# Expert weights in 4 KB rows, 256-column products, a fourth fixed expert and a shared scaling in the second of two transformer blocks

## The chip, the cores and the metric

The kernel runs on one core of a Trainium2 chip. The core has five engines that run their own instruction streams side by side: TensorE (PE in the profile; its weight loads are PEld), VectorE (DVE), ScalarE (ACT), GpSimd (POOL) and SyncE (SP), which here only issues transfers. Sixteen DMA engines move data between main memory and the core's memory. An engine runs its instructions in the order of the program and stops at the first whose inputs or buffer aren't ready. The metric is the device time of one execution in microseconds (us).

## The reference

Two transformer blocks follow one another on 1024 tokens of width 1024, all in float32. Each block is a mixer (attention and others) and a mixture of experts. Only the mixture of the second block matters here. Its routing takes, for each token, the best of four groups and in it the best two of eight experts:

```
grp = argmax(x @ wg + bg);  p_grp = softmax(...)[grp]
e_in = (x @ we + be) of that group          # 8 logits
top_v, top_i = top_k(e_in, 2);  combine = p_grp * softmax(top_v)
for each of its two experts e:              # 32 experts, hidden width 256
    y += combine * ((silu(x @ w_gate[e]) * (x @ w_up[e])) @ w_down[e])
out = h + y                                  # h: the residual
```

w_gate and w_up (w1 and w3 in the code) are 1024 x 256 for each expert, w_down (w2) is 256 x 1024.

## The kernel before, in words

**Precision.** A float32 matrix is split into a high and a low part (`w_split`, L190 on ScalarE and L194 on VectorE for weights; L1835 and L1836 for the tokens), and a product is three products of these: high by high, high by low, low by high. Experts with room for at most 64 tokens (`whole`) put the high and low tokens side by side as 128 columns of the stationary operand, so that two products do; their w2 isn't split at all.

**Experts by size.** The routing sorts the experts by the number of their tokens; position p of that order has room for `caps[p]` rows, written down in a `Lay`. The first NP positions are fixed experts, not sorted ones: their number is known when the program is built, so their weights can be loaded before the routing is known. In the second block NP is 3 with room for 128 each; position 3 has 192, then 128 three times, 96 four times, 80 six times, and 64 fifteen times. `order` says in which order they are computed: 0, 1, 2, and then a large and a small one in turn (3 and 17, 4 and 18, ...), 31 last.

**Weight tiles.** `plan_moe` queues six tiles of 128 x 1024 for each expert: four that hold two rows of 256 of w1 and two of w3 for each partition (two transfers of 256 KB each, with 2 KB contiguous in memory for each partition), and two of w2 (one transfer of 512 KB each, 4 KB contiguous). `w()` hands out the next tile. Before it does, `w_ahead` issues loads for the next LD tiles and splits the next LS. During the last row block of the mixer (`mix_out`) LD grows to 6 NP - 1, so the fixed experts' tiles are all on their way; then LD is 20 and LS is 3. A load of a sorted expert is addressed by a register that SyncE reads from `idx` (L1784), which the routing writes at L1565; SyncE issues in the order of the program, so no load passes that one. The tiles share 42 buffers of 4 KB per partition with the gathered tokens, the split tokens and weights and the outputs.

**One expert.** `gather` (L1809, GpSimd) fetches its tokens' rows. `xT` transposes and splits them. `up` (L1839) takes a tile for each quarter of the contraction and multiplies: each product (L1857) has 512 columns, 256 of w1 and 256 of w3. In the middle of it stands `hT` of the expert before, which transposes its hidden values. SiLU and the product with the other half follow (L1863 to L1869). `down` of the expert before multiplies with w2; ScalarE scales the two halves of the output by the routing weight (L1916), and `put` (L1796) adds the rows to the output with a scatter-add from GpSimd. Four steps of the rest of the routing (`route_rest`) are mixed into each expert until they are done.

**The order** of all this is the order of the program text; each engine's queue is filled by it. What comes first in the loop of `moe` (L1940 to L1957) is: gathers up to five experts ahead, `xT` of the next expert, `up`, the two w2 tiles, `down` of the expert before.

Of the kernel before, what the change touches and what calls it, by code (L numbers as in the profile page):

```python
# [14 lines left out]
OP = mybir.AluOpType  # L15
# [109 lines left out]
class Kern:  # L125
# [1644 lines left out]
    def plan_moe(self, w1, w3, w2, lay, box):  # L1770
        a1 = w1.rearrange("e (p kk k) h -> e kk p (k h)", kk=4, k=2)
        a3 = w3.rearrange("e (p kk k) h -> e kk p (k h)", kk=4, k=2)
        a2 = w2.rearrange("e (k p) d -> e k p d", k=2)
        lo, hi, al = (lambda t: t[:, 0:512]), (lambda t: t[:, 512:1024]), (lambda t: t[:, 0:1024])
        val = {}

        def src(a, p, k):
            if p < lay.NP:
                return a[p, k]

            def go(dst):
                if p not in val:
                    val.clear()
                    val[p] = self.nc.values_load(  # L1784
                        box["r"]["idx"][0:1, 2, p:p + 1], engines=[mybir.EngineType.SP], min_val=0, max_val=lay.E - 1)
                self.sy.dma_start(dst, a[bass.ds(val[p], 1), k].rearrange("o p f -> (o p) f"))
            return go
        for p in lay.order:
            for kk in range(4):
                self.w_add([(lo, src(a1, p, kk)), (hi, src(a3, p, kk))], 1024)  # L1790
            for k2 in range(2):
                self.w_add([(al, src(a2, p, k2))], 1024, None if lay.whole(p) else lay.small > 0 and not lay.add and k2 == 1)


    def put(self, ys, ix, y):
# [3 lines left out]
    def moe(self, r, vs, late=None):  # L1799
        ac, ve, te, gp = self.ac, self.ve, self.te, self.gp  # L1800
        lay = r["lay"]
# [13 lines left out]
        def xT(b):  # L1815
            X[b] = []
            for x, idn, s, n in XG.pop(b):
# [18 lines left out]
                    ve.tensor_sub(xl[:, sl], ps[:, :w], xh[:, sl])  # L1836
                X[b].append((xh, xl, s, n))

        def up(b, mid=None):  # L1839
            U = X.pop(b)  # L1840
            P = [self.p() for _ in U]
            for kk in range(4):
                if kk == 2 and mid is not None:
                    hT(mid)
                wh, wl = self.w()
                next(gen, None)
                for k in range(2):
                    for ps, (xh, xl, s, n) in zip(P, U):
                        c = 2 * kk + k
                        if xl is None:  # L1850
                            ops = [(xh[:, c].rearrange("p j n -> p (j n)"), w) for w in (wh, wl)]
                        else:
                            ops = [(x[:, c * n:(c + 1) * n], w) for x, w in ((xh, wh), (xh, wl), (xl, wh))]
                        m = 2 * n if xl is None else n
                        for j, (x, w) in enumerate(ops):
                            rhs = w[:, :1024].rearrange("p (w k h) -> p w k h", w=2, k=2)[:, :, k, :]
                            te.matmul(ps[:m].rearrange("p (w h) -> p w h", w=2), x, rhs,  # L1857
                                      start=c == 0 and j == 0, stop=c == 7 and j == len(ops) - 1)
            Hn[b] = []
            for ps, (_, xl, s, n) in zip(P, U):  # L1860
                h = self.h()
                if xl is None:
                    ac.activation(h[:n], ps[n:2 * n], AF.Copy)  # L1863
                    ve.tensor_add(h[:n], ps[:n], h[:n])
                    ac.activation(h[:n, 0:256], h[:n, 0:256], AF.Silu)
                    ve.tensor_mul(h[:n, 256:512], h[:n, 0:256], h[:n, 256:512])
                else:
                    ac.activation(h[:n, 0:256], ps[:n, 0:256], AF.Silu)
                    ve.tensor_mul(h[:n, 256:512], h[:n, 0:256], ps[:n, 256:512])  # L1869
                Hn[b].append((h, s, n))  # L1870
# [22 lines left out]
        def down(b):  # L1893
            W = WK.pop(b)
            for t, s, n in HT.pop(b):
                p0, p1 = self.p(), self.p()
                for k in range(2):
                    wh, wl = W[k]
                    if lay.whole(b):
                        m, ops = n, [(t[:, k, :], wh)]  # L1900
                    elif lay.two(b, n):
                        m, ops = 2 * n, [(t[:, k].rearrange("p j n -> p (j n)"), w) for w in (wh, wl)]
                    else:
                        hh, hl = t[:, k, 0, :], t[:, k, 1, :]
                        m, ops = n, ((hh, wh), (hh, wl), (hl, wh))
                    for j, (a, w) in enumerate(ops):
                        f, e = k == 0 and j == 0, k == 1 and j == len(ops) - 1
                        self.mm(p0[:m], a, w[:, 0:512], f, e)
                        self.mm(p1[:m], a, w[:, 512:1024], f, e)
                y = self.t()  # L1910
                for ps, o in ((p0, 0), (p1, 512)):
                    if lay.two(b, n) and not lay.add:
                        ac.activation(y[:n, o:o + 512], ps[n:2 * n], AF.Copy)
                        ve.tensor_add(y[:n, o:o + 512], ps[:n], y[:n, o:o + 512])
                    elif lay.add:
                        ac.activation(y[:n, o:o + 512], ps[:n], AF.Copy, scale=r["wc"][:n, s[1], b:b + 1])  # L1916
                    else:
                        ac.activation(y[:n, o:o + 512], ps[:n], AF.Copy)
                if lay.add:
                    self.put(ys, r["dst"][:n, s[1], b:b + 1], y[:n, :D])  # L1920
                else:
                    gp.dma_start(ys[s[0]:s[0] + n, :], y[:n, :D])

        O = lay.order
        gen = r.pop("gen")
# [11 lines left out]
        for i, b in enumerate(O):  # L1937
# [16 lines left out]
            if i:  # L1954
                down(O[i - 1])
        hT(O[-1])
        down(O[-1])  # L1957
        return ys

# [846 lines left out]
    def run(self):  # L2806
        A = self.A
        l1, l2 = self.lays = (
            Lay(2, [192] * 9 + [128] * 7, [0, 1, 9, 2, 10, 3, 4, 11, 5, 12, 6, 13, 7, 14, 8, 15], 64, False),
            Lay(3, [128] * 3 + [192] + [128] * 3 + [96] * 4 + [80] * 6 + [64] * 15,   # L2810
                [0, 1, 2] + [p + q for p in range(3, 17) for q in (0, 14)] + [31], 64, True))
        b1, b2 = {}, {}
        self.plan_one()
        self.plan_moe(A["exp_w1"][0], A["exp_w3"][0], A["exp_w2"][0], l1, b1)
        self.plan_two()
        self.plan_moe(A["w_gate_2"][0], A["w_up_2"][0], A["w_down_2"][0], l2, b2)
        self.consts()
        self.u_one()
        self.dbg("uT0", self.uh[0].bitcast(F32)[:, NM:NM + T])
        self.attn_one()  # L2820
        self.LD, self.LS = 3, 1
        self.dbg("yc0", self.ycs[0])
        self.conv_pool_in()
        self.mix_load(A["router_g"][0], A["router_e"][0], A["router_g_b"][0], A["router_e_b"][0],
                      A["norm2_g"][0], 16)
        self.merge_one()
        self.uh = self.ul = None
        vs, b1["r"] = self.mix_out(A["x"][0], A["norm2_g"][0], l1, "1")
        def gains():
            self.fg = (self.bcast(A["final_g"], D, self.t()), self.col(A["norm_mix_g_2"][0], 8))  # L2830
        ys = self.moe(b1["r"], vs, gains)
        self.moe_rest(b1["r"], vs, ys, A["exp_w1"][0], A["exp_w3"][0], A["exp_w2"][0])
        self.LS, self.LD = 1, 3
        self.join(b1["r"], ys)
        self.lru()
        self.LD, self.LS = 2, 2
        self.latents()
        self.LD, self.LS = 5, 3
        self.mix_load(A["router_group_w_2"][0], A["router_expert_w_2"][0], A["router_group_b_2"][0],
                      A["router_expert_b_2"][0], A["norm_ffn_g_2"][0], 32)  # L2840
        self.q_kv()
        self.attn_two()
        vs, b2["r"] = self.mix_out(self.x2, A["norm_ffn_g_2"][0], l2, "2", self.out[0])
        ys = self.moe(b2["r"], vs)
        self.moe_rest(b2["r"], vs, ys, A["w_gate_2"][0], A["w_up_2"][0], A["w_down_2"][0])
# [30 lines left out]
```

## Time and profile before

| | |
|---|---|
| time, median of 3 runs | 2680.14 us (2677.69 to 2683.29) |
| the profiled execution | 2676.59 us, of which the span is 2674.5 us |
| mean granted clock of TensorE | 0.97 |
| TensorE, VectorE, ScalarE, GpSimd busy | 93%, 60%, 46%, 23% |
| block two's experts | about 2290 to 2659 us of the span |

Times in the rows are microseconds from the start of the span. A row of a timeline is one or more instructions of one line, with the idle time ahead of them and what ended it in square brackets. In DMA rows `s` is the core's memory, `out<-s,dst` the scatter-add, `s<-vs,idx` the gather, and `in_w_gate`, `in_w_up`, `in_w_down` are the weights. A DMA share is the part of the sixteen engines' time that their packets took; it can be a little over 1. The granted clock is TensorE's, as a share of full speed.

### The profile page before, as it was taken

The page shows a single profiled execution, that of the slowest core. Times are in us where ns is not written, and L with a number is a line of the kernel's source. Part 1 is how long each engine was busy: PE and PEld are TensorE (multiplying, and loading weights), DVE is VectorE, ACT ScalarE, POOL GpSimd, SP SyncE. Part 2 cuts the span into 40 slices and gives each one's busy share as a digit, 9 for nine tenths or more (in the row PEclk, how much of TensorE's full clock was granted, in tenths as well). Part 3 has the DMA queues.
Part 4 walks back from the last instruction along what each step waited for, and adds up shares of the span by engine and source line. Part 5 has one row for each costly group of instructions (what it writes and reads, how often), then busy time and mean ns, then how long its engine had stood idle before and what let it go on. Part 6 is the DMA issues. An engine that isn't in the chain of part 4 may idle for free. (4 is left out here: it accounts for less than half of the span.)

```text
span 2674.5 us, 35232 instructions
## 1 busy us (share of the span) xinstructions
PE 2484.8 (93%) x12192; PEld 1912.6 (72%) x12192; DVE 1596.0 (60%) x2659; ACT 1224.4 (46%) x2153; POOL 608.1 (23%) x661
## 2 busy tenths in 40 slices
PE   7999999999999799959999999998999989689996
PEld 7976696778877577758788888996655567555543
DVE  4235338842245688765754563567776645777775
ACT  4336521131123477755344243435555532457775
POOL 1011111000001234441000002153655622223221
PEclk9999999999999899979999999998999989899998
DMA  4000243223251689852221221333222265789996
GB/s 136 25 9 10 56 144 104 83 83 103 95 181 72 197 291 311 299 195 86 63 87 48 71 79 26 94 123 113 96 96 77 76 211 178 244 249 341 344 347 218
DMA packets 245877, 378.38 MB, mean 141 GB/s; under 512 B 31344, under 2 KB 142224, under 8 KB 245696
## 3 DMA queue, kind: packets, MB, share of 16 engines
q1 hardware_dynamic: 216720, 282.42, 32.6%
q0 software_dynamic: 28976, 93.67, 11.0%
q8 instruction: 98, 1.61, 0.2%
q14 instruction: 83, 0.68, 0.1%
HBM read 296.65 MB, written 81.99 MB: 142 GB/s over the span
## 5 line engine op out<-in xcount | busy, mean ns | idle before, releaser
L216 PE MATMUL ps<-s,s 128*128 128x512 f32 (+15 forms) x8744 | 1922.4, 379 | 37.1 <-ACT s L212 7.2
L216 PEld LDWEIGHTS ps<-s,s 128*128 128x128 f32 (+6 forms) x8744 | 1502.6, 187 | 416.5 <-issue 95.1
L194 DVE TENSOR_TENSOR s<-s,s 128x1024 fp32r<-128x1024 f32 (+4 forms) x375 | 461.7, 1252 | 437.5 <-ACT s L190 402.0
L190 ACT ACTIVATE s<-s 128x1024 fp32r<-128x1024 f32 (+3 forms) x393 | 391.2, 1034 | 73.7 <-DMA s<-in_w_up 16.4
L1857 PE MATMUL ps<-s,s 128*128 128x512 f32 (+3 forms) x1200 | 319.0, 413 | 28.5 <-DVE s L194 23.3
L1857 PEld LDWEIGHTS ps<-s,s 128*128 128x128 f32 (+3 forms) x1200 | 213.8, 186 | 101.4 <-DVE s L194 36.7
L370 DVE TENSOR_REDUCE mx<-ps 128x1 f32<-128x512 f32 (+10 forms) x304 | 142.4, 505 | 17.1 <-PE ps L216 15.3
L504 ACT ACTIVATE s<-ps 128x512 f32<-128x512 f32 (+1 forms) x192 | 93.8, 489 | 114.4 <-PE ps L216 110.6
L1153 ACT ACTIVATE s<-ps 128x512 f32<-128x512 f32 x24 | 14.3, 598 | 252.0 <-PE ps L216 252.0
L519 POOL TENSOR_TENSOR s<-s,s 128x512 f32<-128x512 f32 (+1 forms) x64 | 108.3, 1692 | 48.5 <-ACT s L506 25.4
L1796 POOL DMA_INDIRECT out<-s,dst x33 | 54.0, 1635 | 244.6 <-ACT s L1916 144.5
L466 PE MATMUL ps<-s,s 128*64 128x512 f32 (+3 forms) x384 | 84.4, 521 | 0.8 <-DVE mx L370 0.8
L1046 DVE SCALAR_TENSOR_TENSOR s<-s,c,s 128x1024 f32<-128x1024 f32 x60 | 82.7, 1379 | 1.5
L1809 POOL DMA_INDIRECT s<-vs,idx x58 | 73.3, 1263 | 43.9 <-issue 10.4
L212 ACT ACTIVATE s<-s 128x512 fp32r<-128x512 f32 (+2 forms) x49 | 36.8, 775 | 76.7 <-DVE s L2329 35.6
L434 ACT ACTIVATE s<-ps 128x512 f32<-128x512 f32 (+4 forms) x112 | 49.3, 447 | 47.7 <-PE ps L216 46.6
L213 DVE TENSOR_TENSOR s<-s,s 128x512 fp32r<-128x512 f32 (+2 forms) x49 | 41.8, 890 | 45.5 <-ACT s L212 45.5
L303 ACT ACTIVATE s<-s 128x1024 f32<-128x1024 f32 (+1 forms) x25 | 26.4, 1055 | 89.1 <-DVE s L1316 46.4
L2305 ACT ACTIVATE s<-ps 128x512 f32<-128x512 f32 x16 | 9.6, 598 | 100.9 <-PE ps L216 100.9
L2352 POOL DMA_DIRECT2D g1s<-s x8 | 4.3, 539 | 226.1 <-ACT s L2306 216.9
L192 POOL TENSOR_TENSOR s<-s,s 128x1024 fp32r<-128x1024 f32 x18 | 47.1, 2618 | 32.0 <-ACT s L190 31.9
L1181 POOL DMA_DIRECT2D ms<-s x8 | 4.3, 533 | 215.9 <-DVE s L1148 161.4
(501 smaller groups left out, 2417.2 us busy)
## 6 DMA issues: line engine op xcount, KB each, us to landing
s<-in_w_in SPq DMA_DIRECT2D x80, 512.0 KB
s<-in_exp_w SPq DMA_DIRECT2D x128, 256.0 KB
s<-in_w_gate SPq DMA_DIRECT2D x128, 256.0 KB
s<-in_w_up SPq DMA_DIRECT2D x128, 256.0 KB
s<-in_w_down SPq DMA_DIRECT2D x64, 512.0 KB
s<-in_exp_w SPq DMA_DIRECT2D x32, 512.0 KB
s<-in_x SPq DMA_DIRECT2D x16, 512.0 KB
ms<-s POOLq DMA_DIRECT2D x16, 512.0 KB, 5.0
```

Of the source, the lines that this page charges most:

```text
L190: self.ac.activation(hi[:, :n], st[:, :n], AF.Copy)
L194: self.ve.tensor_sub(lo[:, :n], st[:, :n], hi[:, :n])
L216: self.te.matmul(out, lhsT, rhs, start=start, stop=stop)
L370: self.ve.tensor_reduce(mx[:, ii, j:j + 1], ps[:, c0 - s0:c1 - s0], axis=AX.X, op=OP.max)
L434: self.ac.activation(pf[:rows, c:], s[:rows, c:], AF.Exp)
L466: self.te.matmul(o[64 * hh:64 * hh + 64, c:], H["v"](j)[:rows], pf[:rows, hh, c:], start=first, stop=last and not c, skip_group_check=True)
L504: self.ac.activation(pf[:rows, hh, c:], s[:rows, c:], AF.Exp)
L519: eng.tensor_tensor(acc[:rows, :, c:], acc[:rows, :, c:], pf[:rows, :, c:], op=OP.add)
L1046: ve.scalar_tensor_tensor(a[:, :T], gl[:, k:k + T], cw[:, c, k:k + 1], a[:, :T], op0=OP.mult, op1=OP.add)
L1796: self.gp.indirect_dma_start(out=ys, out_offset=bass.IndirectOffsetOnAxis(ap=ix, axis=0), in_=y, in_offset=None, bounds_check=T - 1, oob_i ...
L1809: gp.indirect_dma_start(out=x[:n, :D], out_offset=None, in_=vs, in_offset=bass.IndirectOffsetOnAxis(ap=r["idx"][:n, j, b:b + 1], axis=0))
L1857: te.matmul(ps[:m].rearrange("p (w h) -> p w h", w=2), x, rhs, start=c == 0 and j == 0, stop=c == 7 and j == len(ops) - 1)
```

## The change

Only the second block is changed, in four places. First, w1 and w3 come in tiles of one matrix each: a transfer of 512 KB, four rows of 256 (4 KB contiguous) for each partition. An expert has six transfers instead of ten, still six tiles, and as many splits. Second, `up_add` takes these tiles in pairs (one of w1, one of w3), so that a pair holds half of the contraction; each product of 512 columns becomes two of 256, one from each tile, and `hT` of the expert before comes after the first pair. Third, four experts are fixed instead of three, each with room for 128; the position with 192 is the fifth, and the order is 0, 1, 2, 3, 17, then (4, 18), (5, 19) and so on, 31 last. Fourth, the second half of a small expert's output is scaled by VectorE from PSUM.

```diff
@@ plan_moe
+        b1, b3 = (w.rearrange("e (p kk k) h -> e kk p (k h)", kk=2, k=4) for w in (w1, w3))
...
         for p in lay.order:
+            if lay.add:
+                for a, n in ((b1, 0), (b3, 0), (b1, 1), (b3, 1), (a2, 0), (a2, 1)):
+                    self.w_add([(al, src(a, p, n))], 1024, None if a is a2 and lay.whole(p) else False)
+                continue
             for kk in range(4):
                 self.w_add([(lo, src(a1, p, kk)), (hi, src(a3, p, kk))], 1024)
             for k2 in range(2):
-                self.w_add([(al, src(a2, p, k2))], 1024, None if lay.whole(p) else lay.small > 0 and not lay.add and k2 == 1)
+                self.w_add([(al, src(a2, p, k2))], 1024, k2 == 1)
@@ moe
+        def up_add(b, U, P, mid):
+            for kk in range(2):
+                if kk and mid is not None:
+                    hT(mid)
+                W = [self.w(), self.w()]
+                for k in range(4):
+                    if k % 2 == 0:
+                        next(gen, None)
+                    c = 4 * kk + k
+                    for ps, (xh, xl, s, n) in zip(P, U):
+                        if xl is None:
+                            m, ops = 2 * n, [(xh[:, c].rearrange("p j n -> p (j n)"), o) for o in (0, 1)]
+                        else:
+                            m, ops = n, [(x[:, c * n:(c + 1) * n], o) for x, o in ((xh, 0), (xh, 1), (xl, 0))]
+                        for j, (x, o) in enumerate(ops):
+                            for h, w in enumerate(W):
+                                self.mm(ps[:m, h * 256:h * 256 + 256], x,
+                                        w[o][:, k * 256:(k + 1) * 256], c + j + h == 0,
+                                        c == 7 and h == 1 and j == len(ops) - 1)
@@ up
+            if lay.add:
+                up_add(b, U, P, mid)
+            else:
...
@@ down
+                    elif o and lay.whole(b):
+                        ve.tensor_scalar(y[:n, o:o + 512], ps[:n], r["wc"][:n, s[1], b:b + 1], None, op0=OP.mult)
                     elif lay.add:
                         ac.activation(y[:n, o:o + 512], ps[:n], AF.Copy, scale=r["wc"][:n, s[1], b:b + 1])
@@ run
-            Lay(3, [128] * 3 + [192] + [128] * 3 + [96] * 4 + [80] * 6 + [64] * 15, 
-                [0, 1, 2] + [p + q for p in range(3, 17) for q in (0, 14)] + [31], 64, True))
+            Lay(4, [128] * 4 + [192] + [128] * 2 + [96] * 4 + [80] * 6 + [64] * 15,
+                [0, 1, 2, 3, 17] + [p + q for p in range(4, 17) for q in (0, 14)] + [31], 64, True))
```

## Rows read from the trace of the kernel before

**Rows 1.** The page's busy time, share and instructions of each engine.

```profile
PE 2484.8 (93%) x12192; PEld 1912.6 (72%) x12192; DVE 1596.0 (60%) x2659; ACT 1224.4 (46%) x2153; POOL 608.1 (23%) x661
```

**Rows 2.** Busy time by window: stretch, engines PE to POOL, granted clock, DMA share, GB/s.

```profile
2287.00:2299.50 12.50, 2.34 (x16) 1.56 (x16) 9.59 (x53) 4.92 (x7) 0.58 (x1) 0.68 0.13 54
...
2310.00:2400.00 90.00, 75.87 (x341) 54.13 (x340) 66.58 (x115) 55.53 (x80) 23.36 (x16) 0.94 0.85 258
2400.00:2530.00 130.00, 122.12 (x548) 76.47 (x547) 103.54 (x131) 100.46 (x145) 37.60 (x26) 1.00 1.03 340
2530.00:2610.00 80.00, 72.30 (x312) 39.69 (x311) 56.49 (x67) 57.86 (x85) 19.86 (x15) 1.00 1.04 347
```

**Rows 3.** SyncE's load issues around the routing: start, duration in us.

```profile
2278.49 1.21 SPq L180 DMA_DIRECT2D s<-in_w_down  x2
2299.91 0.35 SPq L1786 DMA_DIRECT2D s<-in_w_gate  x1
```

**Rows 4.** Chain of waits, the first gather: start, us, what.

```profile
2299.57 6.11 DMA s<-vs,idx
```

**Rows 5.** Chain of waits at the end: the last scatter-add of the loop.

```profile
2654.42 3.52 DMA out<-s,dst
```

**Rows 6.** SyncE's issues from 2383 on.

```profile
2383.49 12.39 SPq L1786 DMA_DIRECT2D s<-in_w_down  x2
2396.79 0.33 SPq L1786 DMA_DIRECT2D s<-in_w_gate  x1
```

**Rows 7.** What SyncE waited for, 2310 to 2410: total us, times, longest.

```profile
SPq L1786 <- DMA out<-s,dst: 11.5, 1, 11.5
```

**Rows 8.** GpSimd's scatter-adds: start, us of the issue, idle before and releaser.

```profile
2470.14 1.47 POOL L1796 DMA_INDIRECT out<-s,dst  x1 [7.10 <-ACT s L1916]
...
2526.56 1.45 POOL L1796 DMA_INDIRECT out<-s,dst  x1 [7.15 <-DMA s<-in_w_up]
...
2609.72 1.42 POOL L1796 DMA_INDIRECT out<-s,dst  x1 [8.68 <-ACT s L1916]
...
2646.90 1.42 POOL L1796 DMA_INDIRECT out<-s,dst  x1 [8.18 <-DVE s L194]
```

**Rows 9.** What the engines waited for, 2530 to 2610: ScalarE's row.

```profile
ACT s L190 <- DMA s<-in_w_up: 14.4, 11, 2.8
```

**Rows 10.** DMA issues 2290 to 2660: count, median us to landing.

```profile
out<-s,dst POOLq DMA_INDIRECT x33, 8.3
```

**Rows 11.** VectorE, around one small expert.

```profile
2496.94 2.36 DVE L194 TENSOR_TENSOR s<-s,s 128x1024 fp32r<-128x1024 f32 x2 [2.02 <-ACT s L1916]
```

**Rows 12.** TensorE, the same expert's last products.

```profile
2501.42 0.97 PE L1857 MATMUL ps<-s,s 128*128 128x512 f32 x3 [0.76 <-DVE s L194]
```

**Rows 13.** DMA, 2629 to 2631: packets and rate, share of the queue.

```profile
DMA packets 448, 0.81 MB, mean 407 GB/s; under 512 B 51, under 2 KB 51, under 8 KB 448
q1 hardware_dynamic: 448, 0.81, 105.6%
```

**Rows 14.** DMA, 754 to 757: the same rows.

```profile
DMA packets 339, 1.26 MB, mean 419 GB/s; under 512 B 32, under 2 KB 32, under 8 KB 339
q1 hardware_dynamic: 339, 1.26, 103.0%
```

**Rows 15.** TensorE, 24 products of 512 columns.

```profile
2355.58 5.79 PE L1857 MATMUL ps<-s,s 128*128 128x512 f32 x24
```

**Rows 16.** ScalarE's evictions between groups of 24 products of 256 columns.

```profile
71.44 0.39 ACT L718 ACTIVATE s<-ps 128x256 f32<-128x256 f32 x1 [2.47 <-PE ps L216]
```

**Rows 17.** TensorE, 96 products of 256 columns.

```profile
1166.21 12.63 PE L216 MATMUL ps<-s,s 128*128 128x256 f32 x96
```

**Rows 18.** ScalarE by form, 2290 to 2675: busy us, mean ns, idle before.

```profile
L1916 ACT ACTIVATE s<-ps,s 64x512 f32<-64x512 f32 x32 | 21.5, 681 | 10.4 <-PE ps L216 10.3
```

**Rows 19.** VectorE by form, the same stretch.

```profile
L1864 DVE TENSOR_TENSOR s<-ps,s 64x512 f32<-64x512 f32 x15 | 10.2, 678 | 3.2 <-ACT s L1863 3.2
```

**Rows 20.** What the engines waited for, 2310 to 2400: VectorE's row.

```profile
DVE s L194 <- DMA out<-s,dst: 12.2, 3, 4.2
```

More of the change, by code (lines that the diff above doesn't have):

```diff
@@ L1841, in up @@
             P = [self.p() for _ in U]
[L1842 to L1858, printed above, removed]
+            if lay.add:
+                up_add(b, U, P, mid)
+            else:
+                for kk in range(4):
+                    wh, wl = self.w()
+                    next(gen, None)
+                    for k in range(2):
+                        for ps, (xh, xl, s, n) in zip(P, U):
+                            c = 2 * kk + k
+                            if xl is None:
+                                ops = [(xh[:, c].rearrange("p j n -> p (j n)"), w) for w in (wh, wl)]
+                            else:
+                                ops = [(x[:, c * n:(c + 1) * n], w) for x, w in ((xh, wh), (xh, wl), (xl, wh))]
+                            m = 2 * n if xl is None else n
+                            for j, (x, w) in enumerate(ops):
+                                rhs = w[:, :1024].rearrange("p (w k h) -> p w k h", w=2, k=2)[:, :, k, :]
+                                te.matmul(ps[:m].rearrange("p (w h) -> p w h", w=2), x, rhs,
+                                          start=c == 0 and j == 0, stop=c == 7 and j == len(ops) - 1)
             Hn[b] = []
```

## The prediction, made before the changed kernel was run

> **What bounds the kernel now.** I read the page's busy shares first: TensorE is busy 2484.8 us of the span [rows 1], so over the whole it is the bound. But the change touches only the experts of block two, so I cut their stretch into windows [rows 2]. There the answer differs. From 2400 to 2530 and from 2530 to 2610 the DMA share is 1.03 and 1.04: the transfers never pause. TensorE is busy 122.12 of 130 and 72.30 of 80 us. Ahead of it stand two stretches in which transfers do pause: 2287 to 2299.5 (share 0.13) and parts of 2310 to 2400 (0.85).
>
> Next the load queue's issues. The last weight load that doesn't depend on the routing is issued at 2278.49, the next at 2299.91 [rows 3]: in between SyncE has nothing to issue, because every later load is addressed by an expert number that isn't there yet. The chain of waits gives the other end of this gap: the first gather starts at 2299.57 and takes 6.11 us [rows 4], while the last scatter-add, with no loads beside it, takes 3.52 us [rows 5]. Both move 128 and 64 rows of 4 KB, so I read the difference as company on the DMA engines: the loads issued from 2299.91 on run beside the gather.
>
> The queue stands still a second time. A w2 load issued at 2383.49 holds it for 12.39 us, until 2396.79, and 11.5 us of that is a wait for a scatter-add to leave its buffer [rows 6, 7]. So every lead that loads had before is gone at 2396.8, and from there one transfer follows the other.
>
> Where TensorE feels it: the scatter-adds of the larger expert of each pair lie at 2470.14, 2526.56, 2609.72, 2646.90 [rows 8], three, four and two pairs apart. That is 18.8 us a pair, then 20.8, then 18.6. In the slow four, ScalarE waits 14.4 us for loads [rows 9]; nothing like it shows for 2400 to 2530, where the lead is being used up. Against 18.8 a pair the four lose 83.2 - 4 x 18.8 = 8.0 us. In the fast pairs what sets the pace is a ring: a scatter-add lands (8.3 us from issue, the median of 33 [rows 10]), frees a buffer, VectorE splits into it (2.36 us, after 2.02 idle), and TensorE's last three products of an expert wait 0.76 us for the next split [rows 11, 12].
>
> **The change part by part.**
>
> *A fourth fixed expert.* 24 tiles instead of 18 are loaded before the routing is known; 3.15 MB at 419 GB/s [rows 14] is 7.5 us moved into the gap, which has about 11 us free. It removes nothing from the total by itself: the load rule is "20 tiles ahead", and from the fourth tile taken on the same tile is asked for at the same point of the program as before. Whatever lead it gives, the queue's standstill at 2383.5 takes back. So 0 for the prefetch as such; its bounds are 0 and, should the lead survive, what the slow four lose beyond the next term. What it does remove is the company of the first gather: its loads are already in. 6.11 - 3.52 = -2.6 us, bounds 0 to -2.6; I take -2.6, since the nearest row (the lone scatter-add) has the same kind of transfer, and everything behind the gather shifts with it. The expert of 192 rows moves two places later in the order; the number of rows computed stays.
>
> *Four rows of 1 KB per partition.* w1 and w3 come in 4 KB runs instead of 2 KB. A stretch with only 2 KB packets of loads ran 407 GB/s at 105.6% of the engines, one with 4 KB packets 419 at 103.0% [rows 13, 14]. For 2.097 MB an expert that saves 2.097/407 - 2.097/419 in thousandths, 0.147 us, by the plain rates; brought to 100% share (385 and 407) 0.294 us. Behind the standstill some 20 experts load until 2610: -2.9 to -5.9 us, and the 8.0 us lost there are the ceiling. I take -4.5. Issues fall from ten to six an expert; SyncE waits for data anyway, so nothing for that.
>
> Here the Trainium skill speaks against the saving: DMA: Bandwidth & Descriptors, Queues, rings and completion order, has each engine drain a whole packet of one ring before it switches to another. The trace so far has scatter-adds landing in 8.3 us beside packets of 2 and 4 KB and in 3.52 alone [rows 5, 10], which agrees with sharing but says nothing of packet size. What it would make of the time is the fourth rival.
>
> *Two 256-column products for one of 512.* 672 products of 512 columns become 1344. The trace has both: 24 products of 512 in 5.79 us, 0.241 each; and groups of 24 products of 256 between two evictions, 0.39 + 2.47 = 2.86 us, 0.119 each [rows 15, 16]. Two make 0.238: -2 us over all. A row of 96 in 12.63 us [rows 17] gives 0.132, +15 us. I take 0, by the first, which is a stream of its own kind as the changed one will be; the second is kept for the range. In the stretch where loads set the pace either is hidden.
>
> *Tiles taken in pairs.* An expert's second half now needs the last split before 8 rather than 4 of its 16 old products. In the ring above that puts a second quarter, 0.97 us [rows 12], behind the split: +0.97 a pair. What stands behind it on TensorE is the down product of the expert before, and with it the scatter-add.
>
> *VectorE scales half of the small experts' output.* ScalarE's 64-row scaling is 0.681 us, VectorE's nearest operation from PSUM 0.678 [rows 18, 19]. Done side by side, the scatter-add is issued up to 0.68 earlier (bounds -0.68 and +0.68 a pair: VectorE's copy may queue behind splits). Together with the pairing I take 0 for the pairs whose pace is set by loads, and for the five exposed ones (three and two [rows 8]) 0.97 - 0.68 + a little queueing, about 0.4: +2 us, bounds 0 and +11.6 (second rival). At the very end the last expert's later half adds 0.97 and the parallel scaling takes 0.68: +0.3.
>
> *Sum.* -2.6 - 4.5 + 0 + 2 + 0.3 = -4.8 us. The profiled execution took 2676.59 us, so 2671.8 in its own terms. It lies 3.5 us below the median of the three runs (2680.14), so 2675.3 as a median.
>
> **The rivals.** A measurement of this kernel can tell about 0.2%, 5.4 us, from no change; 2674.8 and 2685.5 are the borders, and my forecast lies on the lower one.
>
> First, faster: the buffers are handed out in another order, and the load that stood at 2383.5 gets one that is free. Then the lead of 7.5 us survives, the slow four lose nothing (-8.0 instead of -4.5), and of the 12.2 us that VectorE's splits wait for scatter-adds before 2400 [rows 20] half goes. -2.6 - 8.0 - 6.1 + 2.3 = -14.4: 2666. For it: that wait is an accident of one buffer. Against: as many buffers are held as before.
>
> Second, slower: VectorE's scaling stands in its queue behind splits that themselves wait for a scatter-add, so the ring grows by 0.97 + 0.68 = 1.65, from 18.8 to 20.4 a pair. It decides as soon as the scaling starts after ScalarE's half ends. Seven pairs from 2470 to 2609.7 would take 142.8 instead of 139.6 (+3.2), the last two 40.8 instead of 37.2 (+3.6), three larger pairs before them +1.6 each (+4.8). 11.6 - 2.6 + 0.3 = +9.3: 2689. For it: VectorE is busy 103.54 of 130 us [rows 2] and the ring runs through it.
>
> Third, no change: the transfer rate beside scatter-adds and gathers is not the rate of a pure stream, the rows save nothing, and the gather's gain is spent in the ring. 0 to -2: 2679.
>
> Fourth: a scatter-add waits longer behind 4 KB packets. Two thirds of the load bytes come in packets twice as long, so a byte's packet grows by half on average; if the scatter-add's excess over the lone one, 8.3 - 3.5 = 4.8 us, grows as much, that is +2.4 a pair in the ring: 21.2 instead of 18.8. Seven pairs take 148.4 instead of 139.6 (+8.8), the last two 42.4 instead of 37.2 (+5.2), the three larger +7.2; 21.2 - 2.6 + 0.3 = +18.9: 2699.
>
> **How the numbers follow.** Forecast 0.38, its own range 2670 to 2681 and its chance cut in half by the border; first rival 0.22; second 0.23; third 0.12; fourth 0.05. Faster: 0.19 + 0.22 and 0.01 of the third, 0.42. Same: 0.19 + 0.11 = 0.30. Slower: 0.23 + 0.05 = 0.28. The range 2662 to 2691 takes in the first and second rival with a few us of their own spread, and leaves out the fourth and their far ends, some 0.17 together.
>
> **What would show it.** The gap: transfers at some 400 GB/s before 2299 and a first gather near 3.5 us. The rows: a shorter spacing of w2 loads behind 2400 and less waiting of ScalarE for loads in the slow pairs. The standstill at 2383.5: there, elsewhere or gone. The products: 48 of 256 columns in 5.7 us. The ring: fast pairs at 18.8 to 19.2; 20.4 and VectorE's scaling behind a split would be the second rival, a scatter-add median over 10 us the fourth. I am wrong in kind if TensorE's own busy time in block two grows by over 5 us, or if the early stretch changes by more than the gather's 2.6.

## The result, and the profile after

The changed kernel takes 2702.7 us (median of 6 runs, 2700.88 to 2705.8) against 2680.52: the ratio is 1.0081, 95% interval 1.0071 to 1.0091. It is 22 us slower, outside the range of the prediction. Its profiled execution took 2701.23 us, 24.6 more than that of before.

The engines' busy time on the page of the changed kernel, whose span is 2699.4 us:

```profile
PE 2496.5 (92%) x12864; PEld 1971.5 (73%) x12864; DVE 1609.4 (60%) x2674; ACT 1215.6 (45%) x2138; POOL 612.1 (23%) x661
```

The windows of [rows 2] in the changed kernel (the columns are those of the rows):

```profile
2287.00:2299.50 12.50, 2.34 (x16) 1.56 (x16) 9.29 (x52) 4.92 (x7) 0.82 (x2) 0.68 0.58 236
...
2310.00:2400.00 90.00, 74.64 (x477) 65.05 (x475) 65.69 (x110) 51.38 (x73) 19.65 (x14) 0.91 0.78 249
2400.00:2530.00 130.00, 109.12 (x651) 84.62 (x652) 88.11 (x115) 77.04 (x111) 35.76 (x23) 0.91 0.91 293
2530.00:2610.00 80.00, 74.48 (x486) 55.32 (x485) 62.67 (x73) 59.35 (x86) 22.09 (x16) 1.00 1.03 362
```

The gap is used as foretold: its share rises from 0.13 to 0.58. The slow stretch 2530 to 2610 keeps its transfers without a pause (1.03), and TensorE does more in it (74.48 us against 72.30). The loss is in the two windows between. From 2310 to 2400 the DMA share falls from 0.85 to 0.78, and from 2400 to 2530 from 1.03 to 0.91; TensorE is busy 109.12 us of 130 instead of 122.12, at a granted clock of 0.91 instead of 1.00.

What does the same work cost in all? One window from the first gather to the last scatter-add of the loop, first the kernel before, then the changed one:

```profile
2299.57:2654.42 354.85, 315.58 (x1375) 196.42 (x1376) 262.50 (x353) 248.87 (x358) 92.42 (x68) 0.97 0.96 313
```

```profile
2299.26:2679.63 380.37, 329.90 (x2049) 257.70 (x2050) 274.51 (x367) 240.76 (x344) 95.68 (x69) 0.93 0.85 284
```

The stretch is 25.6 us longer. TensorE is idle 50.5 us of it instead of 39.3, 11.2 more, and busy 14.3 us longer for the same columns, at a mean granted clock of 0.93 instead of 0.97. Busy time times clock is the same in both, 315.58 x 0.97 = 306 us and 329.90 x 0.93 = 307. So more than half of the loss isn't waiting as such, but products that ran at a lower clock (the last section shows where the clock fell).

Where in the stretch is it lost? GpSimd's third and eighth scatter-add, the kernel before and then the changed one. The third ends the work on the first three experts. By the eighth both kernels have computed the same seven experts (the one with 192 rows has two scatter-adds):

```profile
2365.50 2.54 POOL L1796 DMA_INDIRECT out<-s,dst  x1 [11.24 <-ACT s L1916]
...
2417.86 1.42 POOL L1796 DMA_INDIRECT out<-s,dst  x1 [6.50 <-ACT s L1835]
```

```profile
2363.78 1.72 POOL L1801 DMA_INDIRECT out<-s,dst  x1 [6.48 <-ACT s L1945]
...
2437.98 2.88 POOL L1801 DMA_INDIRECT out<-s,dst  x1 [11.28 <-DVE s L1841]
```

The changed kernel is 1.7 us ahead at the third and 20.1 us behind at the eighth. So most of the loss falls between about 2364 and 2438 of the changed kernel.

TensorE in the early part of the changed kernel (start, us, instruction, and in brackets the idle time ahead with its releaser):

```profile
2303.66 1.97 PE L1838 MATMUL ps<-c,s 128*128 128x128 f32 x8 [5.64 <-DMA s<-vs,idx]
...
2372.88 0.39 PE L216 MATMUL ps<-s,s 128*128 128x256 f32 x1
2376.21 0.51 PE L216 MATMUL ps<-s,s 128*128 128x256 f32 x2 [2.94 <-ACT s L190]
...
2408.81 0.39 PE L216 MATMUL ps<-s,s 128*128 128x256 f32 x1
2413.08 0.79 PE L216 MATMUL ps<-s,s 128*128 128x256 f32 x2 [3.88 <-ACT s L190]
```

Twice it does the first product of a pair, which needs only the w1 tile, and then stops for ScalarE's half of the split of the w3 tile, 2.94 and 3.88 us. Behind the second stop stands a scatter-add. It is issued at 2399.31, and a split on VectorE starts 10.5 us later, when it has landed. GpSimd's row, then VectorE's, then ScalarE's:

```profile
2399.31 3.98 POOL L1801 DMA_INDIRECT out<-s,dst  x1 [17.43 <-ACT s L1915]
```

```profile
2409.81 1.23 DVE L194 TENSOR_TENSOR s<-s,s 128x1024 fp32r<-128x1024 f32 x1 [7.30 <-DMA out<-s,dst]
2410.95 0.68 DVE L1891 TENSOR_TENSOR s<-ps,s 64x512 f32<-64x512 f32 x1
```

```profile
2411.66 0.42 ACT L1892 ACTIVATE s<-s 64x256 f32<-64x256 f32 x1 [8.33 <-DVE s L1891]
2411.99 1.99 ACT L190 ACTIVATE s<-s 128x1024 fp32r<-128x1024 f32 x2
```

So the wait is handed along: VectorE's next instruction (L1891, which adds the two halves of a small expert ahead of SiLU) stands behind that split, ScalarE waits 8.33 us for it, and the split that TensorE needs comes after that. The first stop has another source. There ScalarE waits 3.90 us for VectorE's L1891 too, but VectorE was busy with steps of the routing ahead of it, not with a wait for a buffer:

```profile
2373.49 0.69 DVE L1691 TENSOR_REDUCE s<-s 128x16 f32<-128x512 f32 x1
2374.09 0.67 DVE L1891 TENSOR_TENSOR s<-ps,s 64x512 f32<-64x512 f32 x1
```

SyncE's load queue shows waits for scatter-adds over the whole stretch (total us, times, longest), the kernel before and then the changed one:

```profile
SPq L1786 <- PE ps L1857: 19.4, 17, 3.4
...
SPq L1786 <- DMA out<-s,dst: 14.1, 2, 11.5
SPq L1786 <- PE ps L216: 8.8, 11, 4.4
```

```profile
SPq L1787 <- DMA out<-s,dst: 63.7, 11, 12.0
SPq L1787 <- PE ps L216: 62.1, 31, 8.3
```

Before, loads stood 14.1 us in two places for a scatter-add to leave its buffer; now 63.7 us in eleven. Waits for TensorE's products to leave a buffer went from 28.2 us (the rows of the two lines together) to 62.1, all on one line now.

The paced stretch, GpSimd's scatter-adds of the larger experts, with the first gather ahead of them:

```profile
2299.26 1.05 POOL L1814 DMA_INDIRECT s<-vs,idx  x1 [6.67 <-DVE idx L1565]
...
2544.10 1.42 POOL L1801 DMA_INDIRECT out<-s,dst  x1 [7.49 <-ACT s L1840]
...
2563.98 1.42 POOL L1801 DMA_INDIRECT out<-s,dst  x1 [7.44 <-ACT s L1840]
...
2583.82 1.42 POOL L1801 DMA_INDIRECT out<-s,dst  x1 [7.44 <-ACT s L1840]
```

They are 19.9 us apart, against 20.8 in the slow pairs before [rows 8] and 18.8 in the fast ones. ScalarE has no row for a wait on loads between 2530 and 2610, where it had 14.4 us [rows 9]. TensorE there stands only for VectorE's half of the pair's second split, 5.5 us in eight places:

```profile
2552.89 2.69 PE L216 MATMUL ps<-s,s 128*80 128x256 f32 x21 [1.00 <-DVE s L194]
```

The loads' packets in these 80 us, the kernel before and then the changed one (packets, MB, share of the sixteen engines):

```profile
q1 hardware_dynamic: 10606, 23.49, 82.3%
```

```profile
q1 hardware_dynamic: 6686, 24.35, 80.5%
```

The changed kernel moves more bytes in a smaller share of the engines' time, 6% more for each part of it.

### The profile page after: what moved, and what is told of

It reads as the page before. It is cut to its first block, busy times and chain, and to the rows that moved or that the text cites. A ratio compares the mean times of both kernels' runs of the same rounds, so it can differ in the third digit from the quotient of the medians.

```text
span 2699.4 us, 36036 instructions
## 1 busy us (share of the span) xinstructions
PE 2496.5 (92%) x12864; PEld 1971.5 (73%) x12864; DVE 1609.4 (60%) x2674; ACT 1215.6 (45%) x2138; POOL 612.1 (23%) x661
## 5 line engine op out<-in xcount | busy, mean ns | idle before, releaser
L216 PE MATMUL ps<-s,s 128*128 128x512 f32 (+16 forms) x10088 | 2115.4, 368 | 75.8 <-DVE s L194 35.8
L216 PEld LDWEIGHTS ps<-s,s 128*128 128x128 f32 (+8 forms) x10088 | 1676.2, 187 | 461.4 <-issue 94.6
L1884 PE MATMUL ps<-s,s 128*128 128x512 f32 x528 | 132.0, 406 | 3.3 <-DVE s L194 1.5
L1153 ACT ACTIVATE s<-ps 128x512 f32<-128x512 f32 x24 | 14.3, 598 | 251.9 <-PE ps L216 251.9
L1884 PEld LDWEIGHTS ps<-s,s 128*128 128x128 f32 x528 | 100.0, 193 | 28.1 <-DVE s L194 2.2
L1814 POOL DMA_INDIRECT s<-vs,idx x58 | 72.0, 1242 | 42.4 <-issue 10.1
```

The source lines that it names most:

```text
L216: self.te.matmul(out, lhsT, rhs, start=start, stop=stop)
L1814: gp.indirect_dma_start(out=x[:n, :D], out_offset=None, in_=vs, in_offset=bass.IndirectOffsetOnAxis(ap=r["idx"][:n, j, b:b + 1], axis=0))
```

## The experiments

All times are medians against the kernel before on the same chip, which was 2680.0 to 2681.6 us. "Stretch" is the time from the first gather to the last scatter-add of the loop in the profiled execution (354.8 us before, 380.4 changed).

| kernel | time, us | ratio, 95% interval | stretch, us |
|---|---|---|---|
| fourth fixed expert alone | 2677.9 | 0.9987 (0.9975 to 0.9998) | 364.8 |
| 4 KB rows in pairs alone | 2700.2 | 1.0069 (1.0052 to 1.0085) | 378.3 |
| VectorE's scaling alone | 2721.5 | 1.0152 (1.0134 to 1.0171) | 401.5 |
| changed, tile by tile | 2719.2 | 1.0146 (1.0129 to 1.0163) | 395.3 |
| before, 17 ahead | 2674.9 | 0.9971 (0.9957 to 0.9986) | 353.2 |
| before, own buffers, 17 ahead | 2696.2 | 1.0052 (1.0037 to 1.0067) | 349.9 |
| changed, own buffers, 17 ahead | 2693.5 | 1.0042 (1.0029 to 1.0054) | 347.7 |
| VectorE's scaling, own buffers, 17 ahead | 2694.5 | 1.0043 (1.0027 to 1.0059) | 349.6 |
| changed, two set aside | 2683.2 | 1.0004 (0.9990 to 1.0018) | 361.2 |
| before, two set aside | 2671.3 | 0.9960 (0.9945 to 0.9975) | 352.6 |
| changed, 17 ahead | 2683.3 | 1.0007 (0.9993 to 1.0020) | 365.2 |
| changed, two set aside, 17 ahead | 2665.5 | 0.9938 (0.9921 to 0.9954) | 344.6 |
| changed, three set aside, 17 ahead | 2668.5 | 0.9955 (0.9940 to 0.9970) | 347.6 |
| changed, three set aside, 14 ahead | 2667.7 | 0.9942 (0.9924 to 0.9959) | 346.4 |
| before, three set aside, 17 ahead | 2666.5 | 0.9947 (0.9929 to 0.9965) | 345.0 |
| changed, tile by tile, three set aside, 17 ahead | 2657.6 | 0.9913 (0.9897 to 0.9930) | 336.6 |

**One part at a time.** Two theories stood at the start: the pairs, and the layout with the fourth fixed expert. The first kernel has only the `Lay(4, ...)` line of the change.

> The kernel before with the fourth fixed expert and its order alone (old tiles, 512-column products, ScalarE scales). The loss of the changed kernel, 22 us, lies before 2425. Pairs theory (a product needs both tiles of a pair split, and the split lead of three tiles is one short): 2676 to 2682, the gather's 1 to 2.6 us gained or lost again. Layout theory (24 tiles and the expert of 192 rows two places later crowd the buffers and stop the load queue): 2690 to 2700.

2677.9: the layout by itself costs nothing; its 2 us are of the size of the gather's. (Its profiled execution, 2684 us, was the longest of its ten, so its stretch is long too.) The second has only the loads and `up_add`:

> The kernel before with 4 KB rows, pairs of tiles and 256-column products alone (three fixed experts, ScalarE scales). Pairs theory: 2692 to 2702, nearly all of the loss, with TensorE waiting for the second tile's split before each pair. Layout theory: 2672 to 2680.

2700.2: the pairs theory holds this far. The waits of that kernel, SyncE's and then ScalarE's, are of the kind seen above:

```profile
SPq L1787 <- DMA out<-s,dst: 43.4, 8, 9.0
```

```profile
ACT s L190 <- PE ps L216: 16.8, 8, 5.8
ACT s L190 <- issue: 15.0, 2, 7.6
```

The third has only this edit:

```diff
+                    elif o and lay.whole(b):
+                        ve.tensor_scalar(y[:n, o:o + 512], ps[:n], r["wc"][:n, s[1], b:b + 1], None, op0=OP.mult)
```

> The kernel before with VectorE scaling the second half of the small experts alone. Both theories: 2678 to 2683, no change that can be told. My second rival (VectorE's scaling queues behind splits): 2688.

2721.5: 41 us slower, more than the whole change, and by none of the theories. The instruction itself can't cost that: 15 of them at some 0.7 us. ScalarE's waits of that kernel, and one of them in its timeline, ahead of it the scatter-add on GpSimd:

```profile
ACT s L190 <- issue: 43.2, 11, 5.6
```

```profile
2477.97 4.02 POOL L1796 DMA_INDIRECT out<-s,dst  x1 [9.98 <-DMA s<-in_w_up]
```

```profile
2488.09 1.06 ACT L190 ACTIVATE s<-s 128x1024 fp32r<-128x1024 f32 x1 [5.06 <-issue]
```

Eleven times ScalarE's half of a split waits for something that the profile doesn't name, in all 43.2 us; the one shown starts 10.1 us after a scatter-add was issued. That it waits for the scatter-add's buffer is an inference at this point. Before, in this place, it was VectorE's half that stood 2.02 us [rows 11]; it comes after ScalarE's, which may be why less hangs on it. The row names ScalarE's scaling as what ended that wait, not a transfer; with two buffers kept for the output rows (below) the 14.9 us that VectorE's splits wait under that name in the kernel before are gone as well.

The fourth undoes the pairs in the changed kernel:

```diff
-                W = [self.w(), self.w()]
-                for k in range(4):
...
-                            for h, w in enumerate(W):
+                for h in range(2):
+                    w = self.w()
+                    for k in range(4):
```

> The changed kernel, but each tile of one matrix is used up before the next is taken: four 256-column columns' worth of products with the w1 tile, then the same with the w3 tile. Loads, layout, number of products and scaling stay. Pairs theory: the lead per tile is that of before again, 2670 to 2682. Layout theory: 2695 to 2703, as the changed kernel.

2719.2, while both theories had it at or below the changed kernel. With that the pairs theory in its plain form fell. What all the slow kernels share is waiting for buffers, at other engines in each: SyncE in the changed kernel and with pairs alone, ScalarE (48.4 us in eleven places, unnamed again) here and with VectorE's scaling. A new theory follows. The 42 shared buffers hold everything, the rows that a scatter-add still reads among them. If the program is laid out with a fixed order in which freed buffers are handed on, any edit shuffles it, and what an edit costs is decided by who is handed the buffer of the scatter-add. No row names a buffer, so this has to be tested by taking the scatter-add's buffers away from the others.

**Buffers of their own for the output rows.** Two buffers outside the shared ones, of which 40 are left; loads go 17 ahead instead of 20, because this does not fit otherwise. The first kernel is the control.

```diff
-MLS, MLP, MLD, MLX = 3, 3, {16: 8, 32: 20}, {16: 2, 32: 5}
+MLS, MLP, MLD, MLX = 3, 3, {16: 8, 32: 17}, {16: 2, 32: 5}
```

> The kernel before with loads 17 tiles ahead instead of 20 in block two, nothing else: the control for the next three. Buffer theory (the time hangs on which engine is handed the buffer that a scatter-add still reads, and any change of the order shuffles that): 2670 to 2700, the sign open. Load theory (less lead, loads pace more): 2684 to 2692.

2674.9: faster, not slower; the load theory is out. (The range of the buffer theory was too wide to be tested by this.) Loads still wait for scatter-adds in it, 12.0 us in two places. The next three add this (and 40 for 42 everywhere):

```diff
+    def ty(self):
+        return self.slab.tile([128, D], F32, name="y4", tag="y4", bufs=2)
...
-                y = self.t()
+                y = self.ty() if lay.add else self.t()
```

> As the control, but the output rows that a scatter-add reads have two buffers of their own, and 40 are left for the rest. Buffer theory: faster than the control and than before, 2650 to 2672, as no split waits for a scatter-add any more. If the ring through the scatter-add isn't the limit: as the control or slower, 2685 to 2700.

> The changed kernel with the two buffers of their own, 40 for the rest and loads 17 ahead. Buffer theory: within 6 us of the kernel before with own buffers. Pairs theory (a product waits for both splits): 15 to 20 us above it.

> The kernel before with VectorE scaling half (alone 41 us slower) and own buffers for the output rows, 40 for the rest, loads 17 ahead. Buffer theory: the 41 us are gone, within 6 us of the kernel before with own buffers. If VectorE's scaling in its queue costs by itself: 30 us or more above it.

2696.2, 2693.5 and 2694.5. The three agree within 3 us: the 41 us of VectorE's scaling are gone, the 22 us of the change too, and no load or split waits for a scatter-add any more in the stretch. How much of the 41 us the loads 17 ahead would give back without own buffers was not run. That the kernels came out slower than before was a miss, and has another place: their first gather is at 2323.9 to 2325.2 instead of 2299.6 (2296.8 in the control), so the 40 shared buffers cost the earlier stages some 25 us. The stretch itself takes 347.7 to 349.9 us; for the kernel before that is 3 us less than in the control (353.2), one execution each.

**Buffers set aside for the stretch only.** To keep 42 for the earlier stages, two (or three) of them are taken when block two's experts begin and used in turn:

```diff
+        YB = [self.t() for _ in range(2)] if lay.add else []
...
-                y = self.t()
+                y = YB.pop(0) if YB else self.t()
+                if lay.add:
+                    YB.append(y)
```

> The changed kernel with one alteration: when block two's experts begin, two of the 42 shared buffers are set aside for the output rows and used in turn; earlier stages keep all 42, loads stay 20 ahead. With own buffers the stretch from the first gather to the last scatter-add took 348 to 350 us in three kernels (380 in the changed one). Buffer theory: 2699.4 - 380 + 348 to 356 in span, so 2668 to 2678 us. If 40 buffers for the rest with loads 20 ahead crowd as before: 2690 to 2705.

> The kernel before with the same two buffers set aside. Buffer theory: 2670 to 2678, a few us below before, and within 5 us of the changed kernel treated likewise, so that the change itself is worth nothing that can be told. If pairs and 4 KB rows matter by themselves: 10 us or more between the two.

2683.2 and 2671.3. The first is above what the buffer theory expected. Setting two aside gives the changed kernel 19.5 of its 22 us back and the kernel before 10. The 63.7 us that its loads waited for scatter-adds are gone, so the scatter-adds' buffers are shown to be a cause; but the two stay 12 us apart, so not the only one. ScalarE's splits in the first 120 us, changed with two set aside, then before with two set aside:

```profile
ACT s L190 <- PE ps L216: 26.3, 12, 6.4
```

```profile
ACT s L190 <- PE ps L1857: 11.1, 8, 3.5
```

Waits of loads and splits for a scatter-add are gone in both; what is left in the changed kernel are split buffers that TensorE still reads. Here a control and a third buffer:

> The changed kernel with loads 17 ahead and shared buffers: the control. Buffer theory: a different order of buffers, 2675 to 2715, no sign foretold. Crowding theory (24 tiles and 20 ahead leave too few buffers): 2675 to 2685.

> The changed kernel with three buffers set aside for the output rows and loads 17 ahead. If the two buffers of the run before still make a scaling wait for the scatter-add two experts back: 3 to 8 us faster than with two. Otherwise the same within 3 us.

2683.3 and 2668.5. Loads 17 instead of 20 ahead, and nothing else, give 19 us too. This alone doesn't tell crowding from order: both ranges held the result, and the waits of loads for scatter-adds fell with it, from 63.7 us to 34.3. With three buffers set aside and loads 17 ahead, ScalarE's wait for TensorE in the first 120 us is down to:

```profile
ACT s L190 <- PE ps L216: 5.4, 6, 1.2
```

The last four were to tell what is crowding and what pairs:

> The changed kernel with two buffers set aside and loads 17 ahead: between 2683.2 (two, 20 ahead) and 2668.5 (three, 17 ahead). Crowding theory: 2668 to 2673, nearly all of the step is the loads ahead. If the third buffer makes it: 2679 to 2684.

2665.5: the step from 2683.2 is the loads ahead, not the third buffer (2668.5). Neither of the two kernels has a load or split that waits for a scatter-add, and ScalarE's wait for TensorE falls from 26.3 us to 4.1. So 17.7 us are a second cause beside the scatter-adds, and crowding is the likely one: with fewer tiles on their way, buffers come free in time. That another order of the buffers did it is less likely, since 14 ahead gives the same:

> The changed kernel with three buffers set aside and loads 14 ahead instead of 17. Crowding theory: the first 150 us get shorter again, 2662 to 2668. If loads 17 ahead already leave enough: the same within 3 us of 2668.5, or slower where loads come late.

2667.7, within 3 us of 2665.5 and 2668.5: 17 ahead leaves enough.

> The kernel before with three buffers set aside and loads 17 ahead. Crowding theory (the change by itself gains the load-paced 8 us once buffers are free): 2673 to 2678, 5 to 10 us behind the changed one. Pairs theory: 2662 to 2668, ahead of it.

2666.5, 2 us ahead of the changed one: inside what the pairs theory expected, but no difference that can be told. With buffers to spare the change as a whole is worth nothing that shows.

> The changed kernel taken tile by tile instead of in pairs (alone 39 us slower than before), with three buffers set aside and loads 17 ahead. Buffer theory: the 39 us vanish, 2664 to 2672. Pairs theory: faster than the pairs' 2668.5 by 4 us or more. If tile by tile costs by itself: above 2680.

2657.6: 11 us ahead of the pairs treated likewise (8 ahead of those with two buffers set aside), 9 ahead of the kernel before. The buffer theory expected less than that; the pairs theory had it. It beats both kernels, by 24 us the one before (0.9913) and by 45 the changed one. TensorE's row for products over the stretch (busy us, mean ns, and idle time before them), pairs first, then tile by tile:

```profile
L216 PE MATMUL ps<-s,s 128*128 128x256 f32 (+7 forms) x1675 | 291.5, 327 | 21.5 <-DVE s L194 16.1 <-ACT s L190 3.8 <-ACT s L1907 0.4
```

```profile
L216 PE MATMUL ps<-s,s 128*128 128x256 f32 (+7 forms) x1674 | 284.9, 324 | 17.7 <-DVE s L194 15.2 <-DVE s L1841 1.1 <-ACT s L190 1.0
```

The pairs cost 6.6 us in TensorE's busy time, at a granted clock of 0.97 against 0.98, and 3.8 in waiting; the wait for ScalarE's half of a split falls from 3.8 us to 1.0 without them. The stretch as a whole, the kernel before and the one tile by tile, each with three buffers set aside and loads 17 ahead:

```profile
2297.92:2642.88 344.96, 312.68 (x1375) 194.72 (x1376) 263.85 (x353) 248.54 (x358) 91.93 (x68) 0.98 0.99 322
```

```profile
2294.12:2630.73 336.61, 312.67 (x2048) 243.81 (x2049) 272.83 (x367) 239.99 (x344) 98.53 (x68) 0.98 0.95 321
```

## Why the prediction was wrong

**The step that failed** is the term in the prediction's sum for the pairing and VectorE's scaling together: +2 us, bounds 0 and +11.6. I priced the ring through the scatter-add as a fixed chain with a named member, VectorE's split, and asked what each edit adds to it. The runs show that the chain is not fixed. With shared buffers, VectorE's scaling alone cost 41 us, though the instruction takes 0.7 us, and the pairs with their rows 20; the wait had moved from VectorE to ScalarE and SyncE. With buffers of their own for the output rows and loads 17 ahead, the scaling cost nothing (2694.5 against 2696.2). The pairs cost 8 to 11 us even with buffers to spare, so that part of the term was too small by itself. The 0 for the fourth fixed expert's prefetch held where it stood alone (2677.9).

The prediction named two signs of being wrong in kind, and both came: TensorE's busy time in block two grew by 14.3 us, where 5 was the limit, and the early stretch changed by more than the gather's 2.6: at the eighth scatter-add the changed kernel is 20.1 us behind.

My first rival had the mechanism ("the buffers are handed out in another order") and gave it only the good sign. The second rival had the sign and 2689, and the wrong cause: VectorE's scaling does start behind a split, but in the paced stretch only 0.2 us after ScalarE's half has ended (2562.49 against 2562.25), and with own buffers and loads 17 ahead it costs nothing.

**Where the 22 us lie.** 19.5 us come back when the scatter-adds have two buffers of their own, 19 us when loads go 17 instead of 20 ahead, and 37 with both (2665.5). So the two add up and give back more than the change had cost; the kernel before gains 15 by both (2666.5 with three buffers). What remains of the change then is two terms: the pairs, +11 us (2668.5 against 2657.6), and the rest, -9 us (2657.6 against 2666.5). The other 20 of the 22 us belong to the way the 42 shared buffers served the changed kernel; how they divide between scatter-adds and crowding stays open. That TensorE's lower clock carries over half of the loss in the changed kernel (14.3 of 25.6 us) was in no term.

**The first gather**: forecast -2.6. Issued at 2299.26, its rows were there when TensorE began at 2303.66: 4.4 us instead of 6.1 [rows 4], so -1.7. Right in kind, and the fourth fixed expert alone measured -2.1. The lone scatter-add that I took for the bound, 3.52 us, moves half as many rows as this gather, so -2.6 was too much to hope for.

**The 4 KB rows and the load-paced pairs**: forecast -4.5 with a ceiling of 8.0. Right in kind: the loads, w2 among them, move 6% more bytes for the same share of the engines (the packets' rows above), where I had estimated 6% for w1 and w3 alone (385 and 407 GB/s). The wait of ScalarE for loads is gone from the stretch where it was 14.4 us [rows 9]. In part that may be because TensorE came later to its tiles: the fastest kernel, tile by tile with buffers set aside, has 22.6 us of it again over its whole stretch. With two buffers set aside the kernel before still waits for loads, the changed one not at all:

```profile
ACT s L190 <- DMA s<-in_w_up: 31.6, 19, 3.2
```

How much of the 9 us that the change gains without pairs are the rows, and how much the earlier start, the runs don't tell apart.

**The standstill** of the load queue at 2383.5 [rows 6] didn't go: in the changed kernel there are eleven such waits in place of two. That lead is lost to it held, but I took one wait for the rule, not for one case of it.

**The 256-column products**: forecast 0. Right: at a granted clock of 0.98 the whole stretch takes 312.68 us of TensorE's time with products of 512 columns and 312.67 with twice as many of 256 (the last two rows of the experiments). The row that gave +15 us [rows 17] came from a stretch at a granted clock of 0.90.

**The fourth rival** is out. Beside 4 KB packets a scatter-add lands no later, 7.8 us against 8.3 [rows 10]:

```profile
out<-s,dst POOLq DMA_INDIRECT x32, 7.8
```

The rule that it was built on (the Trainium skill, DMA: Bandwidth & Descriptors, Queues, rings and completion order: an engine drains a whole packet before it switches) isn't refuted by that. Whether its packets are those that the profile counts, no run here shows.

## What to carry to other kernels

Where buffers are handed on from one shared pool and an asynchronous transfer reads some of them, a kernel's time can hang on who is handed those next: here an edit of 0.7 us cost 41, and one number (20 loads ahead to 17) moved two kernels by 6 and 19. Look first at who waits for the landing of a scatter, at each engine and at the load queue, and give such transfers buffers of their own for the stretch; only then is it worth asking what an edit is worth. And when tiles are split three ahead and taken in pairs, the lead is one tile shorter: taking them one by one gave 8 to 11 us.

## What the runs showed of the hardware

In the changed kernel a wait of some us costs more than its length, because TensorE's clock is lower behind it. TensorE stood 3.57 us ahead of 2328.11. The rows after that, and then one without such a wait ahead of it:

```profile
2328.11 0.32 PE L1647 MATMUL ps<-s 96*128 96x32 bf16 x2 [3.57 <-DVE s L1643]
2328.37 7.40 PE L216 MATMUL ps<-s,s 128*128 128x256 f32 x36
...
2352.80 2.74 PE L216 MATMUL ps<-s,s 128*128 128x256 f32 x21 [0.30 <-DVE s L194]
```

The granted clock (third column from the last) behind the wait, and in the second row:

```profile
2328.10:2330.00 1.90, 1.89 (x11) 1.83 (x12) 0.29 (x1) 0.00 (x0) 0.00 (x0) 0.72 0.29 32
2330.00:2332.00 2.00, 2.00 (x11) 2.00 (x11) 0.00 (x0) 0.00 (x0) 0.00 (x0) 0.50 0.61 234
2332.00:2334.00 2.00, 2.00 (x12) 1.79 (x12) 0.22 (x1) 1.31 (x2) 0.00 (x0) 0.91 0.25 20
...
2352.80:2355.50 2.70, 2.70 (x23) 2.70 (x24) 1.90 (x3) 1.81 (x4) 2.06 (x1) 1.00 1.02 408
```

1.00 is the 2.4 GHz level and 0.50 the 1.2 GHz level. The row of 36 products holds two shapes:

```profile
L216 PE MATMUL ps<-s,s 128*128 128x256 f32 x24 | 4.6, 375 | 0.0
L216 PE MATMUL ps<-s,s 128*128 128x512 f32 x12 | 2.9, 392 | 0.0
```

Its 24 products of 256 columns took 4.6 us, 0.19 each; the 21 at 2352.80 took 0.130 each. Over the stretch with the experts the same columns took 315.6 us of TensorE's time before, 329.9 in the changed kernel and 312.7 in the best, at mean granted clocks of 0.97, 0.93 and 0.98.
